# Unused tiles between weight halves, the halves of transposed h and the arena

## The chip, the cores and the metric

The kernel runs on one core of one Trainium2 chip. The metric is the device time of one execution in microseconds. Three runs of the kernel before took 504.98 us in the median (504.83 to 505.34).

## The reference

One layer of a hybrid decoder block on 512 tokens of width 1024, in float32. A root-mean-square norm is followed by one input projection, whose columns feed two token mixers side by side: native sparse attention (compressed, selected and sliding branches) and multi-scale retention in chunks of 128. Each mixer's output is gated and projected, the two are merged by sigmoid gates, and an output projection with a second norm is added to the input.

```
h = rms_norm(x, norm_pre)
proj = h @ w_in                      # 1024 x 6936, split into 15 parts
o_a = nsa(q_n, k_c, v_c, k_s, v_s, k_w, v_w, gate_n)
y_a = (o_a * silu(z_n)) @ w_nsa_o
o_b = retention(q_r, k_r, v_r)
y_b = (o_b * silu(z_r)) @ w_ret_o
merged = sigmoid(m_a) * y_a + sigmoid(m_b) * y_b
x = x + rms_norm(merged @ w_out, norm_post)
```

## The kernel before, in words

**Split products.** To keep float32 accuracy with TensorE's faster float32r type, each operand is held as two float32r halves, an upper one (`hi`) and a lower one (`lo`, what is left after the upper one). A product is three matmuls: upper by upper, and the two mixed terms. `mm3` issues them in the order `(ah, bh)`, `(ah, bl)`, `(al, bh)`; the first argument is the stationary operand (the weights loaded into TensorE), the second the moving one.

**Weights.** They come from HBM as one stream of 512 KB pieces into a ring of four `raw` tiles. `splitter` makes two pairs `whi`, `wlo` of [128, 512] of each piece, an upper half by a copy (ScalarE or VectorE), a lower half by a subtraction on VectorE. The pairs lie in a pool of their own, `wts`, with nine buffers of each name.

**h.** `hTh` and `hTl` are the halves of the transposed, scaled input, [128, 8, 512] each, in the pool `hT`. They are written at the beginning and at the end overwritten with merged gates.

**The arena.** `arena_r` is one tile of 70 KB per partition in the pool `big`. Most of what is kept as float32r halves lies in it under names given by `at(kb, n, FR)`: the attention's queries, keys and values, the retention's states, the gated outputs `gah`, `gal`, `gbh`, `gbl`. A second region, outside of the pools, holds plain float32 tiles and is named `words`; where the same bytes are used as float32r, their name is `shorts`. Four sums of h's quarters (`SH`) lie in it, but for the lower half of the fourth, which is in the arena at 40 KB.

**Order of allocation in a partition.** Dynamic-DMA scratch and constants, the region of `words`, then the pools `small`, `const`, `wts` (nine `whi`, then nine `wlo`), `hT` (`hTh`, then `hTl`), `big` (`arena_r`, then `rsrow`), `raw`. Each begins where the one ahead of it ends. That puts the first `whi` at byte 69,056, the first `wlo` at 87,488, `hTh` at 105,920, `hTl` at 122,304, `arena_r` at 138,688 and the first `raw` at 212,416: all of them 448 modulo 512. The region of `words` begins at 2,176, which is 128 modulo 512. All larger pieces within these tiles are multiples of 512 bytes, but for the 280 columns of one block (`WC`).

**The matmul loops.** `nat` has h as stationary operand and 512 columns of a weight block as moving one; `tra` has 128 columns of the weights as stationary and h's or a gated output's 512 tokens as moving one. `product` (for the second halves of the merge gates, computed by seven products instead of eight) works with 256 columns: weight slices stationary, quarters of h or their sums `SH` moving. `pair` and `out_seven` are the same for one projection block and for the output. Attention and retention multiply pieces of the arena with each other. Transposes go through TensorE with an identity as moving operand and the data, in `words`, as stationary one (line 263).

**Order of the work.** The order on every engine is written out ahead of time by a planner: coroutines (`od.spawn`) that offer instructions, and a model of the engines' times that picks the next. It depends on modelled costs alone, not on addresses. The tiles' framework derives the semaphores.

Of the kernel before, what the change touches and what calls it, by code (L numbers as in the profile page):

```python
# [10 lines left out]
FT = mybir.dt.float32  # L11
# [7 lines left out]
P = 128  # L19
# [131 lines left out]
def block_kernel(ctx: ExitStack, tc, x, xT, x0s, ws, small, w2s, norm_post, rope_r, dmask, out):  # L151
# [21 lines left out]
    wp = ctx.enter_context(tc.tile_pool(name="wts", bufs=1))  # L173
    hp_ = ctx.enter_context(tc.tile_pool(name="hT", bufs=1))
    bp = ctx.enter_context(tc.tile_pool(name="big", bufs=1))
# [3 lines left out]
    pp = ctx.enter_context(tc.tile_pool(name="ps", bufs=1, space=PSUM))  # L179
    ctx.enter_context(tc.manual_schedule())  # L180

    arena_r = bp.tile([P, 70 * 256], FR, name="arena_r")

    def at(kb, n, dt=FT):
        o = int(kb * 256)
        if dt == FR:
            return arena_r[:, o:o + n]
        assert o + n <= 42 * 256
        return words(kb, n)
# [27 lines left out]
    def copy_ns(o, i, k=0):  # L217
        return (1.042 if far(i) else 0.521) * size(o) + 69 + 61 * k + part(i, 93)
# [4 lines left out]
    def act(o, i, func=AF.Copy, r=0.0, **kw):  # L223
        S.activation(o, i, func, **kw)  # L224
        return od.op("act", act_ns(o, i, lazy(kw.get("bias"), kw.get("scale"))) + (95 if "accum_out" in kw else 0), r)

    def cp_any(o, i, r=0.0):

        cd = copy_ns(o, i)
        if od.begin("act", r) + act_ns(o, i) <= od.begin("dve", r, near(i)) + cd + DVE_BIAS:  # L230
            return act(o, i, r=r)
        V.tensor_copy(o, i)  # L232
        return od.op("dve", cd, r, near(i))
# [50 lines left out]
    nhalf = cp.tile([P, 4], FT, name="nhalf")  # L284
    G.memset(nhalf, -0.5)

    hTh = hp_.tile([P, KD, SEQ], FR, name="hTh")
    hTl = hp_.tile([P, KD, SEQ], FR, name="hTl")


# [124 lines left out]
    def in_ring(p):  # L415

        return min(p, KD) + max(p - 2 * KD, 0) - sum(min(max(p - 2 * i, 0), 2) for i in sload)
    hook = {}

    def load_next():  # L420
        i = len(raws)
        if i < len(loads):
            raw = rp.tile([P, 1024], FT, name="raw", tag="raw", bufs=NR)
            o, c, r = loads[i][0], 0, parts[2 * (i - NR) + 1][2] if i >= NR else 0.0
            for j, n in enumerate(loads[i][1]):
                if isinstance(o, int):
                    DMA.dma_start(raw[:, c:c + n], ws[o:o + P * n].rearrange("(p n) -> p n", p=P))
                    o += P * n
                else:
                    DMA.dma_start(raw, o)  # L430
                e = od.dma(P * n * 4, r)
                c += n
                if i + j == 0:
                    load_xT(0)
            raws.append((raw, e + (EARLY if 6 <= i < 16 else 0.0)))
            for fn in hook.get(i, ()):
                fn()
# [10 lines left out]
    def splitter():  # L448
        for i, (_, pieces) in enumerate(loads):
            n = sum(pieces)  # L450
            for k in range(2):
                p = 2 * i + k
                late = p - 2 * len(loads) + 8
                own = KD <= p < 2 * KD or late >= 0 or i in sload
                if late >= 0:
                    yield od.need("gb")
                if i in sload:
                    yield od.need(*{2: ("heads",), 1: ("vr0", "vr1"), 0: ("pair1",), 3: ("pair2",)}.get(sload[i], ("sums",)))
                yield lambda: own or in_ring(p) < in_ring(len(done)) + NW
                while len(raws) <= i:  # L460
                    yield lambda: len(raws) > i or len(raws) < NR or len(parts) > 2 * (len(raws) - NR) + 1
                    if len(raws) <= i:
                        load_next()
                r = max(raws[i][1], done[-1] if done and not own else sfree.get(sload.get(i), 0.0))
                yield r, "act"
                m = n // 2
                src = raws[i][0][:, k * m:(k + 1) * m]
                if late >= 0:
                    hi, lo = at(4 * late, 512, FR), at(4 * late + 2, 512, FR)
                elif i in sload:  # L470
                    hi, lo = (a[:, k * 512:(k + 1) * 512] for a in SB[sload[i]])
                elif own:
                    hi, lo = WC[p - KD]
                else:
                    hi = wp.tile([P, 512], FR, name="whi", tag="whi", bufs=NW)
                    lo = wp.tile([P, 512], FR, name="wlo", tag="wlo", bufs=NW)
                vh, vl = hi[:, :m], lo[:, :m]
                if sload.get(i, 0) % 10 == 1:
                    e = act(vh, src, r=r, scale=-1.0)
                elif p:  # L480
                    e = cp_any(vh, src, r)
                else:
                    V.tensor_copy(vh, src)
                    e = od.op("dve", copy_ns(vh, src), r, True)
                od.spawn(split_lo(p, hi, lo, src, vh, vl, e), rank(p))
                nxt[0] = p + 1
                yield

    def split_lo(p, hi, lo, src, vh, vl, r):
        yield lambda: rank(p)() == 0 or od.eng["dve"] <= od.now + SLACK  # L490
        yield r
        if sload.get(p // 2, 0) % 10 == 1:
            r = stt(vl, src, -1.0, f(vh), OP.mult, OP.subtract, r)
        else:
            r = sub_split(vl, src, vh, r)
        yield lambda: len(parts) == p
        parts.append((hi, lo, r))
        if p % 2 and len(raws) <= p // 2 + NR:
            load_next()
# [3 lines left out]
    def rank(p):  # L503

        return lambda: 0 if p <= wanted[0] + (PSOON if p in pairp else SOON) else 4
# [1364 lines left out]
    od.spawn(h_split(), 0)  # L1870
    od.spawn(norms(), 1)
    od.spawn(splitter(), lambda: rank(nxt[0])())
    od.spawn(edges(), 1)
    od.spawn(weight_sums(), 1)
# [111 lines left out]
```

## Time and profile before

| | |
|---|---|
| median of three runs | 504.98 us |
| the profiled execution | 504.99 us, span 503.2 us |
| TensorE (PE) | 493.7 us busy, 98%, 2666 matmuls |
| TensorE weight loads (PEld) | 421.4 us, 84% |
| VectorE (DVE) | 424.6 us, 84% |
| ScalarE (ACT) | 324.7 us, 65% |
| GpSimd (POOL) | 39.3 us, 8% |
| HBM | 249 GB/s over the span |

A row of the table of groups gives line, engine, operation, names (written tile, arrow, read tiles), shapes, count, then busy us, mean ns of one, and idle time ahead of it with what ended it. Matmuls are pipelined and their spans overlap: the mean of one is longer than the step from one start to the next. A row of the timeline gives start and length in us, engine, line, operation, names, shape, and how many instructions are merged in the row.

### The profile page before, as it was taken

The page shows a single profiled execution, that of the slowest core. Times are in us where ns is not written, and L with a number is a line of the kernel's source. Part 1 is how long each engine was busy: PE and PEld are TensorE (multiplying, and loading weights), DVE is VectorE, ACT ScalarE, POOL GpSimd, SP SyncE. Part 2 cuts the span into 40 slices and gives each one's busy share as a digit, 9 for nine tenths or more (in the row PEclk, how much of TensorE's full clock was granted, in tenths as well). Part 3 has the DMA queues.
Part 4 walks back from the last instruction along what each step waited for, and adds up shares of the span by engine and source line. Part 5 has one row for each costly group of instructions (what it writes and reads, how often), then busy time and mean ns, then how long its engine had stood idle before and what let it go on. Part 6 is the DMA issues. An engine that isn't in the chain of part 4 may idle for free.

```text
span 503.2 us, 7872 instructions
## 1 busy us (share of the span) xinstructions
PE 493.7 (98%) x2666; PEld 421.4 (84%) x2666; DVE 424.6 (84%) x996; ACT 324.7 (65%) x722; POOL 39.3 (8%) x66
## 2 busy tenths in 40 slices
PE   8999999999999999999999999999999999999994
PEld 7898887888888888888888888888888989988883
DVE  6698899989989989998789999778787867979795
ACT  6795599558679788784587574835435535527642
POOL 3102100023000210000100000101000000000010
PEclk9999999999999999999999999999999999999999
DMA  8968995779998899325556673530473735635813
GB/s 318 385 211 283 326 227 200 242 136 225 370 238 182 262 293 211 113 85 166 119 173 212 215 235 114 126 126 8 162 250 113 233 116 191 199 113 169 303 56 142
DMA packets 31080, 98.75 MB, mean 196 GB/s; under 512 B 3136, under 2 KB 6976, under 8 KB 30272
## 3 DMA queue, kind: packets, MB, share of 16 engines
q1 hardware_dynamic: 24576, 70.85, 41.5%
q0 software_dynamic: 6320, 27.26, 22.9%
q8 instruction: 21, 0.34, 0.3%
q14 instruction: 19, 0.16, 0.1%
q10 hardware_dynamic: 144, 0.14, 0.1%
HBM read 93.52 MB, written 31.98 MB: 249 GB/s over the span
## 4 chain that ended last, share of the span: by engine, by line
PE 89%; DMA 5%; DVE 4%; issue 1%; ACT 0%; POOLq 0%; DVEq 0%; POOL 0%; ACTq 0%; SPq 0%
PE bank L257 70%; PE bank L1234 8%; PE bank L1725 7%; PE bank L263 4%; DMA raw<-in_stream_dram 3%; DVE arena_r L236 1%; DMA words<-in_xT_dram 1%; DVE wlo L236 1%; DMA words<-in_x_dram 1%; DVE words L236 1%; DVE words L679 0%; DVE words L249 0%; DVE words L243 0%; DVE words L967 0%; DVE whi L232 0%
## 5 line engine op out<-in xcount | busy, mean ns | idle before, releaser
L224 ACT ACTIVATE whi<-raw 128x512 fp32r<-128x512 f32 x177 | 107.0, 627 | 53.4 <-PE bank L257 36.2
L236 DVE TENSOR_TENSOR wlo<-raw,whi 128x512 fp32r<-128x512 f32 x188 | 123.4, 685 | 10.4 <-ACT whi L224 9.5
L257 PE MATMUL bank<-whi,hTh 128*128 128x512 f32 x192 | 74.0, 407 | 0.3 <-ACT hTh L224 0.3
L257 PE MATMUL bank<-arena_r 128*128 128x256 f32 (+2 forms) x328 | 70.7, 335 | 0.7 <-DVE arena_r L236 0.5
L257 PE MATMUL bank<-whi,hTl 128*128 128x512 f32 x192 | 71.2, 391 | 0.0
L257 PE MATMUL bank<-wlo,hTh 128*128 128x512 f32 x192 | 71.0, 390 | 0.0
L224 ACT ACTIVATE arena_r<-bank 128x512 fp32r<-128x512 f32 (+3 forms) x104 | 49.1, 476 | 26.3 <-PE bank L263 25.4
L236 DVE TENSOR_TENSOR arena_r<-bank,arena_r 128x512 fp32r<-128x512 f32 (+3 forms) x104 | 56.0, 542 | 9.6 <-ACT arena_r L224 8.5
L257 PE MATMUL bank<-arena_r,whi 128*128 128x512 f32 (+1 forms) x208 | 63.6, 381 | 0.0
L224 ACT ACTIVATE words<-words,stat 128x128 f32<-128x128 f32 (+3 forms) x105 | 54.1, 546 | 6.6 <-DVE stat L967 4.9
L257 PEld LDWEIGHTS bank<-arena_r 128*128 128x128 f32 x328 | 50.8, 189 | 7.6 <-DVE arena_r L236 1.2
L257 PE MATMUL bank<-hTh,whi 128*128 128x512 f32 (+1 forms) x144 | 52.2, 363 | 0.0
L257 PE MATMUL bank<-hTh,wlo 128*128 128x512 f32 (+1 forms) x144 | 51.4, 357 | 0.0
L257 PE MATMUL bank<-hTl,whi 128*128 128x512 f32 (+1 forms) x144 | 51.1, 355 | 0.0
L257 PEld LDWEIGHTS bank<-arena_r,whi 128*128 128x128 f32 x208 | 38.8, 188 | 7.3
L257 PEld LDWEIGHTS bank<-whi,hTl 128*128 128x128 f32 x192 | 36.2, 188 | 8.0
L257 PEld LDWEIGHTS bank<-whi,hTh 128*128 128x128 f32 x192 | 36.5, 191 | 6.9 <-ACT hTh L224 0.6
L257 PEld LDWEIGHTS bank<-wlo,hTh 128*128 128x128 f32 x192 | 36.1, 188 | 6.3
L257 PE MATMUL bank<-arena_r,wlo 128*128 128x512 f32 x96 | 37.3, 389 | 0.0
L263 PEld LDWEIGHTS bank<-identr,shorts 128*128 128x128 f32 x268 | 30.1, 140 | 8.6 <-DVE arena_r L236 0.9
L224 ACT ACTIVATE words<-words 128x512 f32<-128x512 f32 (+3 forms) x47 | 27.2, 586 | 12.8 <-DVE words L236 8.0
L263 PE MATMUL bank<-identr,shorts 128*128 128x128 f32 x268 | 31.6, 238 | 0.5 <-DVE arena_r L236 0.5
(182 smaller groups left out, 891.0 us busy)
## 6 DMA issues: line engine op xcount, KB each, us to landing
raw<-in_stream_dram SPq DMA_DIRECT2D x73, 512.0 KB, 4.4
pair<-in_stream_dram POOLq DMA_DIRECT2D x6, 1024.0 KB, 11.8
t<-in_stream_dram POOLq DMA_DIRECT2D x6, 1024.0 KB, 17.2
out<-in_stream_dram POOLq DMA_DIRECT2D x6, 1024.0 KB, 17.1
words<-in_x_dram SPq DMA_DIRECT2D x8, 512.0 KB, 6.9
raw<-s SPq DMA_DIRECT2D x8, 512.0 KB, 4.2
raw<-pair SPq DMA_DIRECT2D x8, 512.0 KB, 4.2
raw<-t SPq DMA_DIRECT2D x8, 512.0 KB, 3.6
```

The costliest lines, as they stand in the source:

```text
L224: S.activation(o, i, func, **kw)
L236: (V if e == "dve" else G).tensor_tensor(o, a, b, op=op)
L257: T.matmul(ps, a, b, start=start, stop=stop)
L263: T.transpose(ps, a, idn)
L1234: T.matmul(ps[m], a, b, start=n in first and s + j == 0, stop=n in last and s + j == 5, skip_group_check=True)
L1725: T.matmul(ps[m], a, b, start=n in first and s + i == 0, stop=n in last and s + i == 5, skip_group_check=True)
```

## The change

It allocates tiles that nothing writes or reads, so that what is allocated behind them begins elsewhere: 64 bytes per partition between the `whi` and the `wlo`, 128 ahead of `hTh`, 128 between `hTh` and `hTl`, 128 ahead of `arena_r`. Modulo 512, `whi` stays at 448, `wlo` moves to 0, `hTh` to 128, `hTl` to 256, `arena_r`, `rsrow` and `raw` to 384; `words` stays at 128. All other text of the kernel is the same. `spacer` allocates once per pool, however often it is called.

```diff
+    spaced = set()
+
+    def spacer(pool, n):
+
+        if pool not in spaced:
+            spaced.add(pool)
+            pool.tile([P, n], FT, name=f"room{n}")
+
+    spacer(bp, 32)
     arena_r = bp.tile([P, 70 * 256], FR, name="arena_r")
...
+    hp_.tile([P, 32], FT, name="room_h")
     hTh = hp_.tile([P, KD, SEQ], FR, name="hTh")
+    spacer(hp_, 32)
     hTl = hp_.tile([P, KD, SEQ], FR, name="hTl")
...
                     hi = wp.tile([P, 512], FR, name="whi", tag="whi", bufs=NW)
+                    spacer(wp, 16)
                     lo = wp.tile([P, 512], FR, name="wlo", tag="wlo", bufs=NW)
```

## The prediction

> **What bounds the kernel now.** I read the page first, from busy shares to the chain of work that ended last, then the table of groups by shape, then the timeline of TensorE alone.
>
> ```profile
> PE 493.7 (98%) x2666; PEld 421.4 (84%) x2666; DVE 424.6 (84%) x996; ACT 324.7 (65%) x722; POOL 39.3 (8%) x66
> PEclk9999999999999999999999999999999999999999
> PE 89%; DMA 5%; DVE 4%; issue 1%; ACT 0%; POOLq 0%; DVEq 0%; POOL 0%; ACTq 0%; SPq 0%
> ```
>
> TensorE is busy 98% of the span at full granted clock and carries 89% of the chain, so the time is the sum of the steps from one matmul to the next. The change adds no instruction, wait or transfer; it can only alter how long instructions take. So the question is whether any instruction's time depends on where its operand starts. In a row, the first name behind the arrow is the moving operand, the second the stationary one.
>
> Where tiles start, worked out from the sizes in order of allocation, in bytes of a partition modulo 512: words and shorts 128; whi, wlo, hTh, hTl, arena and raw all 448. After: words 128, whi 448, wlo 0, hTh 128, hTl 256, arena and raw 384.
>
> The vector engines first, since they already mix starts of 128 and 448:
>
> ```profile
> L236 DVE TENSOR_TENSOR wlo<-raw,whi 128x512 fp32r<-128x512 f32 x188 | 123.4, 685 | 10.4 <-ACT whi L224 9.5 <-PE bank L257 0.4
> L236 DVE TENSOR_TENSOR arena_r<-words,arena_r 128x512 fp32r<-128x512 f32 x15 | 10.1, 682 | 0.0
> L224 ACT ACTIVATE whi<-raw 128x512 fp32r<-128x512 f32 x177 | 107.0, 627 | 53.4 <-PE bank L257 36.2 <-DMA raw<-in_stream_dram 8.2 <-DMA raw<-pair 2.2
> L224 ACT ACTIVATE words<-words 128x512 f32<-128x512 f32 x27 | 16.9, 627 | 5.9 <-DVE words L236 2.8 <-DVE words L249 2.7 <-PE bank L263 0.2
> ```
>
> Three operands at 448 take VectorE 685 ns, a mixture of 128 and 448 takes 682; ScalarE takes 627 in both. I cost the change at nothing there, and these engines have idle time beside TensorE anyway. If that is off by the 3 ns shown, 188 of them are 0.6 us of VectorE time under cover of TensorE; without that cover they would show.
>
> TensorE is another matter. The same shape, 128x256, has two prices:
>
> ```profile
> L257 PE MATMUL bank<-hTh,wlo 128*128 128x256 f32 x48 | 13.6, 283 | 0.0
> L257 PE MATMUL bank<-hTl,whi 128*128 128x256 f32 x48 | 13.6, 282 | 0.0
> L257 PE MATMUL bank<-hTh,whi 128*128 128x256 f32 x48 | 13.6, 282 | 0.0
> L257 PE MATMUL bank<-shorts,whi 128*128 128x256 f32 x112 | 21.0, 277 | 0.0
> L257 PE MATMUL bank<-shorts,wlo 128*128 128x256 f32 x64 | 17.7, 277 | 0.0
> L257 PE MATMUL bank<-arena_r,whi 128*128 128x256 f32 x16 | 4.5, 281 | 0.0
> L257 PEld LDWEIGHTS bank<-shorts,whi 128*128 128x128 f32 x112 | 17.5, 188 | 0.0
> ```
>
> All are issued by `product`, with the same weight slices and kind of output; only the moving operand's place differs. While one matmul streams, the next one's weights are loaded (188 ns), so what can collide is the moving read with the load of the *next* weights. The steps, from the timeline of TensorE (start us, us):
>
> ```profile
> 387.02 0.28 PE L257 MATMUL bank<-hTl,whi 128*128 128x256 f32 x1
> ...
> 388.94 0.28 PE L257 MATMUL bank<-hTh,wlo 128*128 128x256 f32 x1
> ...
> 394.70 0.39 PE L257 MATMUL bank<-shorts,whi 128*128 128x256 f32 x2
> ...
> 395.72 0.39 PE L257 MATMUL bank<-shorts,whi 128*128 128x256 f32 x2
> ...
> 404.05 0.28 PE L257 MATMUL bank<-shorts,whi 128*128 128x256 f32 x1
> ...
> 406.06 0.28 PE L257 MATMUL bank<-shorts,wlo 128*128 128x256 f32 x1
> ```
>
> First pair: moving hTh or hTl at 448, weights at 448, distance 0: 16 steps in 1.92 us, 120.0 ns each. Second pair: shorts at 128, weights at 448, distance 192: 9 steps in 1.02 us, 113.3 ns. Third pair: the fourth weight sum, whose upper half is in words (128) and lower half in the arena (448), so that distances run 192, 0, 192: 17 steps in 2.01 us, 118.2 ns. So distance matters by 6.7 ns, and a sequence that changes distance costs more than the mean of its parts: (2 x 113.3 + 120.0) / 3 = 115.5, measured 118.2, a surcharge of 2.7 ns; over the clean step it is 4.9.
>
> The 512-column matmuls, which are most of the time:
>
> ```profile
> 359.81 0.39 PE L257 MATMUL bank<-arena_r,wlo 128*128 128x512 f32 x1
> ...
> 361.85 0.39 PE L257 MATMUL bank<-arena_r,wlo 128*128 128x512 f32 x1
> 219.72 0.46 PE L263 MATMUL bank<-identr,shorts 128*128 128x128 f32 x4
> 220.02 0.46 PE L257 MATMUL bank<-whi,hTh 128*128 128x512 f32 x1
> 220.32 0.39 PE L257 MATMUL bank<-wlo,hTh 128*128 128x512 f32 x1
> ...
> 222.40 0.39 PE L257 MATMUL bank<-wlo,hTh 128*128 128x512 f32 x1
> ```
>
> At distance 0 throughout, a long run makes 9 steps in 2.04 us: 226.7 ns, twice 113.3, so with no stall left. Right after four transposes (shorts at 128 as weights) the same matmuls make 9 steps in 2.08 us, and only then settle. A run of one distance settles into a clean step; a break in it costs some 0.04 us.
>
> **The change part by part.** *No instruction moves.* A spacer tile is allocated and never touched. Every queue keeps its order; POOL's and SP's DMAs are the same. *The raw tiles* shift by 448 bytes; the page's row for them stays my price:
>
> ```profile
> raw<-in_stream_dram SPq DMA_DIRECT2D x73, 512.0 KB, 4.4
> ```
>
> They still start at a multiple of 64, and the ring runs ahead of the splits, so I cost that at nothing; if a landing became later, ScalarE's splits would be late next (DMA is 5% of the chain).
>
> *Distances after the change*, moving start minus start of the next weights, modulo 512. `nat` (moving whi, wlo, whi; weights hTh, hTh, hTl): 0, 0, 0 becomes 320, 256, 320. `tra` on hTh and hTl: 0, 0, 0 becomes 192, 256, 192. `tra` on the gated halves in the arena: 448, 384, 448. `product` on hTh and hTl: 192, 256, 192; on the first three weight sums: from 192 throughout to 192, 128, 192; on the fourth: from 192, 0, 192 to 192, 384, 192. Attention keeps both operands in the arena, at distance 0. So the constant distance of the 512-column runs, the condition under which they settle, becomes an alternating one. How many they are:
>
> ```profile
> L257 PE MATMUL bank<-whi,hTh 128*128 128x512 f32 x192 | 74.0, 407 | 0.3 <-ACT hTh L224 0.3
> L257 PE MATMUL bank<-hTh,whi 128*128 128x512 f32 x96 | 38.7, 403 | 0.0
> L257 PE MATMUL bank<-arena_r,whi 128*128 128x512 f32 x192 | 59.2, 389 | 0.0
> L257 PE MATMUL bank<-arena_r,wlo 128*128 128x512 f32 x96 | 37.3, 389 | 0.0
> ```
>
> Each of the first two rows stands for a product in three parts (upper by upper, upper by lower, lower by upper): 3 x 192 + 3 x 96 + 192 + 96 = 1152 (the first block's 96, four of one kind in a row, alternate less often; I count them in).
>
> - 512 columns, 1152 of them, now alternating. Bounds: 0 (they settle at 226.7 as before) and 4.9 ns each (the fourth sum against the clean one), 5.6 us; below nothing, the unsettled stretches could go, which is the second rival. I take half the surcharge of 2.7, since a 512-column step leaves room for the 188 ns load that a 113 ns step doesn't: 1.35 x 1152 = +1.6 us.
> - `product` on hTh and hTl, 144 matmuls: from 120.0 towards the fourth sum's pattern, 118.2 if distance 256 acts as 0 does: -0.3 us (113.3 would be -1.0).
> - The first three weight sums, 176 - 32 = 144 matmuls: between 113.3 and 118.2, the middle: +0.35 us (0 to +0.7).
> - The fourth sum, 16 + 32 = 48: loses its zero; 0 to -4.9 ns, the middle: -0.1 us.
> - Attention's arena-by-arena matmuls and the transposes: unchanged.
>
> Sum +1.6. The profiled execution took 504.99 us (span 503.2, so 1.8 outside, which stays), the median of the runs is 504.98: 504.99 + 1.6 = 506.6 us. TensorE's share of the chain, 89%, would take 0.2 off, which I leave in. What a run can tell from no change is about 0.2%, 1.0 us.
>
> The Trainium skill, SBUF — State Buffer, "Who interferes with whom", says that the moving operand and LDWEIGHTS have independent read ports and that TensorE and ScalarE never wait on anyone. By that rule the sum is 0 and the time 505.0. The trace disagrees as far as TensorE goes (120.0 against 113.3 ns at one shape) and agrees for ScalarE (627 and 627 ns).
>
> **The rivals.** *Likeliest, slower:* alternating distance keeps runs from settling, +1.6 us as summed; at the fourth sum's full 4.9 ns, +5.6 + 0.7 - 0.3 = +6.0, 511.0 us. For it speaks the third timeline pair; against it that it was measured at 256 columns only.
>
> *No change:* the 512-column runs settle with alternating distances too, since only the first few steps of a run collide; `product` gives 0.3. 504.7 us. For it speaks that after transposes, whose weights lie elsewhere, nine steps suffice. The rule of ports comes out here as well.
>
> *Faster:* distance 0 is the only bad one, and 256 is as good as 192. Then `product` on hTh and hTl goes to 113.3 (144 x 6.7 = -1.0 us), and runs start settled. The transposes are
>
> ```profile
> L263 PE MATMUL bank<-identr,shorts 128*128 128x128 f32 x268 | 31.6, 238 | 0.5 <-DVE arena_r L236 0.5
> ```
>
> about 67 fours, 67 x 0.04 = 2.7 us at most; half of it, because attention's runs stay at 0: -1.35. Together -2.4, 502.6 us; at most -3.7, 501.3. For it speaks the second pair; against it the third, where a zero in three costs more than its third. It decides from the point where alternating costs a 512-column matmul under 0.3 ns.
>
> **How the numbers follow.** Alternation costs: 0.42, of which 0.06 stays within 0.2%. No change: 0.27. Faster: 0.27. Something else of either sign (landings, the vector engines): 0.04, shared. That makes faster 0.28, same 0.34, slower 0.38. Range: from below the faster case, 502.0, to most of the full surcharge, 510.0; the likeliest case alone runs from 505.5 to 511.0.
>
> **What would show it.** Right: `product` on hTh and hTl near 118 ns a step; the long 512-column run near 360 us at 228 instead of 226.7; mean durations of those groups up from 389. The no-change rival: 226.7 there again. The faster one: 113.3 in `product`, and nine steps after transposes in 2.04 us. VectorE at 685 and ScalarE at 627 in each case; another number there makes my reading of the vector engines wrong. The sum would be wrong in size if attention's arena matmuls changed, which I cost at nothing.

## The result and the profile after

Three runs of the changed kernel took 509.58 us in the median (508.69 to 509.6), against 504.98: 1.0084 times as long, 95% interval 1.0061 to 1.0107. Five more runs, told of below, gave 1.0076 (1.0063 to 1.009). The change costs some 4 us. (A ratio is worked out from the single runs of both kernels, so it can differ a little from the quotient of the medians.) One run of e12 below fell to a granted clock of 0.56 and took 811.68 us; it is left out of that kernel's numbers. The profiled execution took 508.69 us, its span is 506.9 us, 3.7 more than before.

The page of the changed kernel, the busy times, the granted clock and the chain's shares by engine:

```profile
PE 497.2 (98%) x2666; PEld 421.2 (83%) x2666; DVE 425.2 (84%) x996; ACT 325.2 (64%) x722; POOL 39.1 (8%) x66
...
PEclk9999999999999999999999999999999999999998
...
PE 91%; DVE 4%; ACT 2%; issue 1%; DMA 1%; DVEq 0%; POOLq 0%; POOL 0%; ACTq 0%
```

TensorE is busy 3.5 us longer with the same 2666 matmuls. The granted clock does not explain it: its mean is 0.998 before and 0.996 after, and in the group of runs around e11 below the kernel before took 504.99 us at 0.996, the changed one 509.27 us at 0.999. TensorE's weight loads (421.4 before), VectorE (424.6) and ScalarE (324.7) hardly move. The groups by shape (nine lines were added ahead of them, so L257 is now L266, L236 is L245, L224 is L233):

```profile
L245 DVE TENSOR_TENSOR wlo<-raw,whi 128x512 fp32r<-128x512 f32 x188 | 123.7, 685 | 10.2 <-ACT whi L233 9.1 <-PE bank L266 0.4
L233 ACT ACTIVATE whi<-raw 128x512 fp32r<-128x512 f32 x177 | 107.1, 627 | 52.9 <-PE bank L266 37.4 <-DMA raw<-in_stream_dram 5.4 <-PE bank L1246 2.1
...
L266 PE MATMUL bank<-whi,hTh 128*128 128x512 f32 x192 | 73.8, 404 | 0.4 <-ACT hTh L233 0.4
...
L266 PE MATMUL bank<-arena_r,whi 128*128 128x512 f32 x192 | 60.2, 394 | 0.0
...
raw<-in_stream_dram SPq DMA_DIRECT2D x73, 512.0 KB, 4.5
```

VectorE stays at 685 ns, ScalarE at 627, the weight stream's landing at 4.5 us (4.4 before). Among the matmuls some means rise (389 to 394), some fall (407 to 404): a mean holds the pipelined overlap and the waits at breaks. The steps from start to start say more. Three long stretches serve as gauges in all that follows: 48 matmuls of `product` on hTh and hTl, then 72 on the first three sums of h's quarters (`SH`; the prediction calls them weight sums, here they are "the sums"), and later 96 on the gated halves in the arena. TensorE's timeline of the kernel before, the first row of each stretch and the first row behind it:

```profile
386.55 0.28 PE L257 MATMUL bank<-hTh,whi 128*128 128x256 f32 x1
...
392.30 0.29 PE L257 MATMUL bank<-shorts,whi 128*128 128x256 f32 x1
...
400.48 0.28 PE L257 MATMUL bank<-hTh,whi 128*128 128x256 f32 x1
...
436.67 0.39 PE L257 MATMUL bank<-arena_r,whi 128*128 128x512 f32 x1
...
458.43 0.39 PE L1725 MATMUL bank<-whi,arena_r 128*128 128x512 f32 x1
```

and of the changed kernel, with two rows from the long 512-column stretch near 365 us ahead:

```profile
364.31 0.39 PE L266 MATMUL bank<-arena_r,wlo 128*128 128x512 f32 x1
...
366.39 0.39 PE L266 MATMUL bank<-arena_r,wlo 128*128 128x512 f32 x1
...
388.81 0.28 PE L266 MATMUL bank<-hTh,whi 128*128 128x256 f32 x1
...
394.37 0.28 PE L266 MATMUL bank<-shorts,whi 128*128 128x256 f32 x1
...
402.87 0.28 PE L266 MATMUL bank<-hTh,whi 128*128 128x256 f32 x1
...
439.27 0.62 PE L266 MATMUL bank<-arena_r,whi 128*128 128x512 f32 x2
...
461.45 0.62 PE L1737 MATMUL bank<-whi,arena_r 128*128 128x512 f32 x2
```

`product` on hT: 5.75 us by 48 is 119.8 ns before, 5.56 us is 115.8 after. The sums: 8.18 us by 72 is 113.6, now 8.50 us, 118.1. The gated halves: 21.76 us by 96 is 226.7, now 22.18 us, 231.0; near 365 us nine steps take 2.08 us, 231.1 each, where they took 2.04. Those steps repeat as 229, 236, 228 to the end of the stretch and do not settle.

A step runs from one matmul's start to the next one's and so holds any wait between them. Adding the steps of all matmuls by kind, after less before, places the whole 3.7 us of the span: 512 columns through `mm3` (1152) +2.13; 512 columns issued in `pair` and `out_seven` with weights as moving operand (288) +1.19; all four sums +0.66; `product` on hT -0.53; attention's arena matmuls -0.05; all else +0.29. The +2.13 is a net: over the steps under 250 ns, `nat` goes from 228.5 to 230.7 ns in the mean, `tra` on hT from 229.6 to 231.6, the gated halves from 226.7 to 231.1, together +3.0 us, while the longer steps, which hold the waits and breaks, came out 0.9 us shorter.

### The profile page after: what moved, and what is told of

Same layout as the page of the kernel before. It is cut to its first block, busy times and chain, and to the rows that moved or that the text cites. A ratio compares the mean times of both kernels' runs of the same rounds, so it can differ in the third digit from the quotient of the medians.

```text
span 506.9 us, 7872 instructions
## 1 busy us (share of the span) xinstructions
PE 497.2 (98%) x2666; PEld 421.2 (83%) x2666; DVE 425.2 (84%) x996; ACT 325.2 (64%) x722; POOL 39.1 (8%) x66
## 4 chain that ended last, share of the span: by engine, by line
PE 91%; DVE 4%; ACT 2%; issue 1%; DMA 1%; DVEq 0%; POOLq 0%; POOL 0%; ACTq 0%
PE bank L266 73%; PE bank L1246 8%; PE bank L1737 7%; PE bank L272 4%; DVE arena_r L245 1%; ACT words L233 1%; DVE wlo L245 1%; DMA words<-in_x_dram 1%; DVE words L245 1%; DVE words L979 0%; ACT whi L233 0%; DVE words L691 0%; ACT arena_r L233 0%; DVE words L258 0%; DVE words L252 0%
## 5 line engine op out<-in xcount | busy, mean ns | idle before, releaser
L233 ACT ACTIVATE whi<-raw 128x512 fp32r<-128x512 f32 x177 | 107.1, 627 | 52.9 <-PE bank L266 37.4
L245 DVE TENSOR_TENSOR wlo<-raw,whi 128x512 fp32r<-128x512 f32 x188 | 123.7, 685 | 10.2 <-ACT whi L233 9.1
L266 PE MATMUL bank<-whi,hTh 128*128 128x512 f32 x192 | 73.8, 404 | 0.4 <-ACT hTh L233 0.4
L266 PE MATMUL bank<-whi,hTl 128*128 128x512 f32 x192 | 71.8, 394 | 0.0
L266 PE MATMUL bank<-arena_r 128*128 128x256 f32 (+2 forms) x328 | 70.7, 335 | 0.6 <-DVE arena_r L245 0.5
L266 PE MATMUL bank<-wlo,hTh 128*128 128x512 f32 x192 | 71.2, 391 | 0.0
L233 ACT ACTIVATE arena_r<-bank 128x512 fp32r<-128x512 f32 (+3 forms) x104 | 49.1, 477 | 27.1 <-PE bank L272 26.1
L245 DVE TENSOR_TENSOR arena_r<-bank,arena_r 128x512 fp32r<-128x512 f32 (+3 forms) x104 | 56.0, 541 | 10.7 <-ACT arena_r L233 9.5
L266 PE MATMUL bank<-arena_r,whi 128*128 128x512 f32 (+1 forms) x208 | 64.6, 386 | 0.0
L233 ACT ACTIVATE words<-words,stat 128x128 f32<-128x128 f32 (+3 forms) x105 | 54.1, 545 | 6.7 <-DVE stat L979 4.9
L266 PEld LDWEIGHTS bank<-arena_r 128*128 128x128 f32 x328 | 50.9, 189 | 7.6 <-DVE arena_r L245 0.8
L266 PE MATMUL bank<-hTh,whi 128*128 128x512 f32 (+1 forms) x144 | 52.2, 363 | 0.0
L266 PE MATMUL bank<-hTl,whi 128*128 128x512 f32 (+1 forms) x144 | 51.2, 355 | 0.0
L266 PE MATMUL bank<-hTh,wlo 128*128 128x512 f32 (+1 forms) x144 | 51.0, 354 | 0.0
L266 PEld LDWEIGHTS bank<-arena_r,whi 128*128 128x128 f32 x208 | 38.9, 188 | 7.6
L266 PEld LDWEIGHTS bank<-whi,hTl 128*128 128x128 f32 x192 | 36.0, 188 | 8.5
L266 PEld LDWEIGHTS bank<-whi,hTh 128*128 128x128 f32 x192 | 35.9, 188 | 7.2 <-ACT hTh L233 0.7
L266 PEld LDWEIGHTS bank<-wlo,hTh 128*128 128x128 f32 x192 | 36.2, 189 | 6.8
L266 PE MATMUL bank<-arena_r,wlo 128*128 128x512 f32 x96 | 37.6, 392 | 0.0
L233 ACT ACTIVATE words<-words 128x512 f32<-128x512 f32 (+3 forms) x47 | 27.2, 586 | 12.7 <-DVE words L245 7.7
```

The costliest lines, as they stand in the source:

```text
L245: (V if e == "dve" else G).tensor_tensor(o, a, b, op=op)
L266: T.matmul(ps, a, b, start=start, stop=stop)
```

## Experiments

Two theories stood at the start. A, the prediction's: a constant distance between moving operand and next weights lets a run settle, an alternating one doesn't. B: at 512 columns every distance but 0 costs, constant or not. Each kernel below is the kernel before with the edit shown. Beside them the kernel before took 505.1, 505.35, 505.29 and 505.2 us in the four groups of runs; a ratio is against the runs of its group, with its 95% interval. Distances from here on are modulo 256, for a reason that the third experiment gives.

**One constant distance of 192 (e1).**

```diff
+    hp_.tile([P, 48], FT, name="room_h")
     hTh = hp_.tile([P, KD, SEQ], FR, name="hTh")
```

> One spacer of 192 bytes ahead of hTh and no other: whi and wlo stay at 448, hTh, hTl, arena and raw move to 128 modulo 512, where words lies already. Distances (moving start minus start of the next weights) are then constant within each loop: nat 320, tra and product 192, attention 0. Theory A (what costs is a distance that alternates from one matmul to the next): the long 512-column run of the gated halves settles at 226.7 ns a step, product on hTh and hTl goes from 120.0 to 113.3 ns (144 matmuls, -1.0 us), the fourth sum from 118.2 to 113.3 (-0.2 us): about 503.8 us, below the kernel before. Theory B (any distance other than 0 costs a 512-column matmul): 1152 matmuls at some +4.4 ns, less 1.2 us at 256 columns: about 509 us.

508.07 us, ratio 1.0062 (1.0049 to 1.0074). Its timeline, the same gauges:

```profile
389.73 0.28 PE L257 MATMUL bank<-hTh,whi 128*128 128x256 f32 x1
...
395.18 0.28 PE L257 MATMUL bank<-shorts,whi 128*128 128x256 f32 x1
...
403.34 0.28 PE L257 MATMUL bank<-hTh,whi 128*128 128x256 f32 x1
...
439.02 0.62 PE L257 MATMUL bank<-arena_r,whi 128*128 128x512 f32 x2
...
461.41 0.62 PE L1726 MATMUL bank<-whi,arena_r 128*128 128x512 f32 x2
```

At the constant distance of 192, `product` on hT falls to 113.5 ns (5.45 us by 48), as hoped for 256 columns. The gated halves, at the same constant 192, rise to 233.2 (22.39 us by 96), more than in the changed kernel with its mixture. Theory A falls, B stands. What is best for 256 columns is bad for 512. A fourth stretch is used from here on, 48 matmuls of `out_seven` with h's tiles as stationary operand and weights as moving one, as in `nat`. In e1 they stand at a constant 64:

```profile
466.92 0.39 PE L1726 MATMUL bank<-whi,hTh 128*128 128x512 f32 x1
...
477.90 0.39 PE L1726 MATMUL bank<-whi,arena_r 128*128 128x512 f32 x1
```

10.98 us by 48 is 228.8 ns, where the kernel before took 226.7.

**Only the 64 bytes between whi and wlo (e2).**

```diff
                     hi = wp.tile([P, 512], FR, name="whi", tag="whi", bufs=NW)
+                    if not spaced:
+                        spaced.append(wp.tile([P, 16], FT, name="room_w"))
                     lo = wp.tile([P, 512], FR, name="wlo", tag="wlo", bufs=NW)
```

> Only the 64 bytes between whi and wlo: whi at 448, wlo, hTh, hTl, arena and raw at 0. nat has 448, 0, 448; tra and the gated halves 64, 0, 64; the first three weight sums 192, 128, 192. Theory A (alternation): all 1152 pay as in the changed kernel, some +4.4 ns each, sums +0.7 us: 509 to 510 us. Theory B (distance other than 0): two of three pay, about +3.4 us, sums +0.7: 509 us, but the step at distance 0 stays 226.7. Rival C (the spacing of h and the arena is what costs, the weight halves are harmless): 505 us.

509.86 us, ratio 1.0096 (1.0081 to 1.0112). One spacer of 64 bytes costs as much as all four spacers of the change. All that is allocated behind it shifts by 64 as well, so that of three matmuls on the gated halves two stand at 64 and one at 0 (229.3 ns on average), and in `nat` and the stretch of `out_seven` two at 192 and one at 0:

```profile
467.38 0.40 PE L1728 MATMUL bank<-whi,hTh 128*128 128x512 f32 x1
...
478.63 0.40 PE L1728 MATMUL bank<-whi,arena_r 128*128 128x512 f32 x1
```

11.25 us by 48 is 234.4 ns. Both theories had given about this time; that the weight halves would be harmless falls.

**256 bytes at the same place (e3).** The same edit with 64 words instead of 16.

> 256 bytes between whi and wlo in place of 64: whi at 448, wlo, hTh, hTl, arena and raw at 192. nat has 256, 0, 256; tra and the gated halves 256, 0, 256; sums 192, 448, 192. If the pattern of places repeats every 256 bytes, 256 is as 0: the 512-column runs settle at 226.7, product on hTh and hTl stays at 120.0, and only the sums pay, at most +0.7 us: 505.0 to 505.7 us. If it repeats every 512 bytes or later, theory A gives 509 to 510 us, as with 64 bytes.

504.9 us, ratio 0.9995 (0.9986 to 1.0004). The gated halves in its timeline:

```profile
436.48 0.62 PE L258 MATMUL bank<-arena_r,whi 128*128 128x512 f32 x2
...
458.24 0.62 PE L1728 MATMUL bank<-whi,arena_r 128*128 128x512 f32 x2
```

21.76 us, 226.7 ns. An unused tile as such costs nothing, and a distance of 256 is as good as 0: the pattern repeats every 256 bytes as far as this shows.

**Only the 128 bytes between hTh and hTl (e4).**

```diff
     hTh = hp_.tile([P, KD, SEQ], FR, name="hTh")
+    hp_.tile([P, 32], FT, name="room_l")
     hTl = hp_.tile([P, KD, SEQ], FR, name="hTl")
```

> Only 128 bytes between hTh and hTl: whi, wlo, hTh at 448, hTl, arena and raw at 64. nat has 0, 384, 0; tra on h 0, 128, 0; the gated halves 128 throughout; first three sums 192 throughout as before. Theory A (alternation): nat and tra on h pay, 864 x 4.4 ns = 3.8 us, the long run of the gated halves settles at 226.7: about 508.5 us. Theory B (distance other than 0): the gated halves pay (288 x 4.4), and one in three of nat and tra (288 x 4.4): +2.5 us, 507.5 us, with the long run of the gated halves near 231.

510.13 us, ratio 1.0101 (1.0087 to 1.0114). The arena shifts with it: gated halves at a constant 128 take 233.3 ns. Theory B had given 507.5: `pair` and `out_seven`, which it did not count, add 1.5 us by the steps, the sums 0.7, and the gated halves cost 0.6 more than reckoned. Its timeline has one thing that no theory asked for:

```profile
389.59 0.28 PE L257 MATMUL bank<-hTh,whi 128*128 128x256 f32 x1
...
395.24 0.28 PE L257 MATMUL bank<-shorts,whi 128*128 128x256 f32 x1
...
403.72 0.28 PE L257 MATMUL bank<-hTh,whi 128*128 128x256 f32 x1
```

`product` on hT, now at 0, 128, 0, takes 117.7 ns. The sums behind it stand where they stood, at a constant 192, and still take 117.8 (8.48 us by 72) instead of 113.6.

**All tiles from the weights on moved together by 64, words not (e5).**

```diff
+    wp.tile([P, 16], FT, name="room_w")
     arena_r = bp.tile([P, 70 * 256], FR, name="arena_r")
```

> One spacer of 64 bytes ahead of whi: whi, wlo, hTh, hTl, arena and raw all move together, from 448 to 0 modulo 512; words stays at 128. All distances among them stay 0, only the weight sums go from 192 to 128. Relative theory (the price of a 512-column matmul goes by the distance modulo 256 of moving operand and next weights, 0 being free): 512-column runs settle at 226.7 as before, the first three sums leave 113.3 for at most 120: 505.0 to 506.0 us. Absolute theory (the place itself counts, 448 being the good one): 512-column steps rise as in the changed kernel, 509 us.

505.67 us, ratio 1.0002 (0.9993 to 1.0012). The rows of the sums and of the gated halves:

```profile
393.58 0.28 PE L258 MATMUL bank<-shorts,whi 128*128 128x256 f32 x1
...
402.13 0.28 PE L258 MATMUL bank<-hTh,whi 128*128 128x256 f32 x1
...
438.74 0.40 PE L258 MATMUL bank<-arena_r,whi 128*128 128x512 f32 x1
...
460.51 0.39 PE L1726 MATMUL bank<-whi,arena_r 128*128 128x512 f32 x1
```

At distance 0 the gated halves stay at 226.8 ns although whi, wlo, h's halves and the arena all lie elsewhere; the sums, whose distance went from 192 to 128, take 118.8. It is the distance that counts, not the place.

**Only the 128 bytes ahead of the arena (e6).**

```diff
+    bp.tile([P, 32], FT, name="room_a")
     arena_r = bp.tile([P, 70 * 256], FR, name="arena_r")
```

> Only the 128 bytes ahead of the arena: whi, wlo, hTh, hTl stay at 448, arena and raw at 64 modulo 512. nat and tra on h keep distance 0, the gated halves have 128 throughout, attention 0, the first three sums 192 with the addresses of before. Relative theory: only the gated halves (288 at some +6.6 ns) and the merged gates with weights (about 140 at some +5) pay: +2.6 us, 507.6 us; nat stays at 226.7. On the sums, which run at 117.7 ns in the kernel with 128 bytes between hTh and hTl although their addresses are those of before: if what came ahead of them (a product at alternating distance) is the cause, 113.3 here; if the place of raw and arena, and so the traffic of the other engines, is, 117.7 here too.

509.12 us, ratio 1.006 (1.0042 to 1.0079). Gated halves at 128: 233.3 ns (22.40 us by 96). The stretch of `out_seven` with h's tiles, untouched, ran 226.9. The time expected was 507.6. The gated halves, `pair` and `out_seven` cost 2.7 us by the steps, as reckoned; another 1.2 us of its profile lie in the first 96 matmuls of `nat`, which keep distance 0. They ran from 4.89 to 28.84 us instead of 4.71 to 27.42, and why stays open. The sums took 113.6 here, so the arena's place was not what slowed them in e4. What differs there is the stretch ahead of them, `product` at mixed distances.

**Constant 32 and constant 224 (e7, e8).** As in e1, with 8 and with 56 words.

> One spacer of 32 bytes ahead of hTh: distances constant, tra, product and the gated halves +32, nat -32, attention 0, sums as before. If the price grows evenly with distance between 0 (nothing) and 64 (nat at 229.0 ns, +2.3): about +1.2 ns on 1152, 506.4 us. If half a line of 64 bytes is worse than a whole one (the single weight load 32 bytes off in the kernel before is followed by a step of 235): +8 ns on 1152, 514 us.

> One spacer of 224 bytes ahead of hTh: distances constant, tra, product and the gated halves 224 modulo 256 (that is -32), nat +32. The mirror image of the kernel with 32 bytes. If only the size of the distance counts, the same time as there; if its sign counts too (192 costs 6.8 ns, 64 only 2.3), nat and tra change places and the times differ: the loops at +32 would be the cheaper ones.

511.39 us, ratio 1.0115 (1.01 to 1.013), and 511.37 us, 1.0113 (1.0096 to 1.0131). The gated halves at 32:

```profile
441.66 0.62 PE L257 MATMUL bank<-arena_r,whi 128*128 128x512 f32 x2
...
464.05 0.63 PE L1726 MATMUL bank<-whi,arena_r 128*128 128x512 f32 x2
```

22.39 us, 233.2 ns; 233.3 at 224. The smallest step away from 0 that was tried costs the full price, in either direction; neither 506.4 nor 514 us, the times expected for e7, came out.

**Words at distance 0 too, the sums kept at 192 (e9).** The prediction laid the unsettled steps after transposes on the transposes' weights, which lie elsewhere. If so, this should beat both kernels.

```diff
-    nc.alloc_sbuf_tensor("room", [P, 58 * 256], FT)
-    low, made = nc.sbuf_base - 58 * 1024, {}
+    nc.alloc_sbuf_tensor("room", [P, 58 * 256 + 64], FT)
+    low, made = nc.sbuf_base - 58 * 1024 - 192, {}
...
-        v = [words(4 * i, 1024, FR) for i in range(7)] + [at(40, 1024, FR)]
+        v = [words(4 * i - 1 / 16, 1024, FR) for i in range(7)] + [at(40, 1024, FR)]
```

> The region of words moves 64 bytes up, everything behind it by 256, so that words come to distance 0 from all other tiles (modulo 256); the weight sums alone are taken 64 bytes lower, which keeps them at distance 192. Nothing else changes. Distance 0 as the free one for 512 columns: the matmuls that stream while the weights of a transpose (words) load now take 230 to 238 ns and come down to 226.7, some 68 x 7 ns = -0.5 us, and the runs after transposes start settled, up to -2.7 us: 502.2 to 504.8, most likely 504. If the load of a transpose's weights unsettles a run for another reason than its place (its 128 columns, its PSUM bank): 505.3, no change. Weight sums at 113.3 ns by both.

505.14 us, ratio 0.9999 (0.999 to 1.0008). No gain. Its timeline, nine steps after four transposes at two places, from the second matmul at the first and from the third at the other (from the second it is 2.08 us there, too):

```profile
220.06 0.40 PE L257 MATMUL bank<-wlo,hTh 128*128 128x512 f32 x1
...
222.10 0.39 PE L257 MATMUL bank<-wlo,hTh 128*128 128x512 f32 x1
...
270.55 0.40 PE L1234 MATMUL bank<-wlo,arena_r 128*128 128x512 f32 x1
...
272.63 0.39 PE L1234 MATMUL bank<-wlo,arena_r 128*128 128x512 f32 x1
```

2.04 us at the first place, where the kernel before took 2.08; 2.08 at the second, where the kernel before took 2.04 by its steps. At the 23 places where at least eleven 512-column matmuls follow transposes, these nine steps take 2.065 us in the mean before and 2.068 here. So the place of the transposes' weights is not what unsettles a run. A break does it without any transpose: behind twelve 256-column matmuls of attention, all in the arena, the kernel before takes 236, 228, 233 and 230 ns from 240.43 us. Whether the place of the identity, which streams in a transpose, adds to it isn't tested; e9 leaves it as it was against all tiles but words.

**The same tiles as in e5 moved by 192 (e10).** With 48 words instead of 16: words come to distance 0, and the sums with them.

> 192 bytes ahead of the first weight tile: all tiles but words move by 192 and come to distance 0 from words, the weight sums included. Weight sums from 113.3 to 120.0 ns: 144 x 6.7 = +1.0 us and the fourth sum from 118.2 to 120.0, +0.1. With the gain at transposes as in the run beside it (-0.5 to -2.7 us): 503.8 to 506; without it 506.4. If the sums stay at 113.3, a distance of 0 at 256 columns isn't what costs 120.0, and the place of hTh and hTl is.

506.85 us, ratio 1.003 (1.0018 to 1.0041), 1.6 us more than before. The sums:

```profile
392.92 0.28 PE L258 MATMUL bank<-shorts,whi 128*128 128x256 f32 x1
...
401.56 0.28 PE L258 MATMUL bank<-hTh,whi 128*128 128x256 f32 x1
```

8.64 us by 72 is 120.0 ns: distance 0 is the costly one at 256 columns, in words as in hT. By the steps of its profile the sums cost +1.0 us, as foreseen. Its first 60 us hold 0.5 us more of waits than before, which no distance explains; the reason stays open.

**The changed kernel in more rounds (e11), and a constant 128 (e12).** e12 is e1 with 32 words.

> The changed kernel again, in more rounds, so that its price is known to better than 1 us: by the steps of its profile (226.7 to 232 ns and mixtures of 229 on 1152 matmuls, product and sums as measured) 509.0 to 509.6 us, ratio 1.0085. Is the distance the only cause, its unsettled runs look the same again: 229 to 236 ns near 365 us.

> 128 bytes ahead of hTh, all else as before: one constant distance of 128 modulo 256 in every 512-column product with weights or h, and in product on hTh and hTl. If only distance 0 is free at 512 columns: 233.3 ns everywhere in them, 1152 x (233.3 - 228) = +6.1, product on hT near 119, sums 113.3 as before: 511.3. If the place of the arena or alternation carries part of the price (the kernels with one spacer of 128 cost 3.0 and 5.1 us): 508 to 510.

The changed kernel: 509.19 us, ratio 1.0076 (1.0063 to 1.009), gated halves 231.0 ns again. Its second profile has a span of 507.4 us, and the 1152 matmuls of `mm3` take +2.79 us there, against +2.13 in the first; `pair` and `out_seven` +1.18, sums +0.67, `product` -0.53; the steps under 250 ns of the 1152 cost +3.0 us as in the first. The constant 128: 510.53 us, ratio 1.0105 (1.009 to 1.0121).

```profile
391.03 0.28 PE L257 MATMUL bank<-hTh,whi 128*128 128x256 f32 x1
...
396.73 0.28 PE L257 MATMUL bank<-shorts,whi 128*128 128x256 f32 x1
...
441.39 0.62 PE L257 MATMUL bank<-arena_r,whi 128*128 128x512 f32 x2
...
463.78 0.63 PE L1726 MATMUL bank<-whi,arena_r 128*128 128x512 f32 x2
```

`product` on hT 118.8 ns, gated halves 233.2. A constant distance of 128 costs more than the change's mixture of 192, 128 and 192 does in the same stretch.

## Why the prediction was right or wrong

It said slower by 1.6 us, and the kernel is slower by some 4. That it gets slower, that TensorE's steps alone do it, and that `product` on hT gains while the 512-column matmuls and the first three sums lose, held. The size and the mechanism did not. The direction was luck in part: by the prediction's mechanism a constant distance would have cost nothing, and constant distances of 32, 128 and 224 cost more than the change does (e7, e12, e8). The change slows the kernel because most distances it makes at 512 columns are not 0. The range had room for 509.58 us only because it allowed for most of the full surcharge.

- *The count.* 1152 left out 288. In `pair` and `out_seven`, 512-column matmuls are issued by lines of their own, not through `mm3`. The groups of the changed kernel:

```profile
L1246 PE MATMUL bank<-whi,arena_r 128*128 128x512 f32 x64 | 20.4, 399 | 0.0
L1246 PE MATMUL bank<-wlo,arena_r 128*128 128x512 f32 x32 | 12.5, 392 | 0.0
L1737 PE MATMUL bank<-whi,arena_r 128*128 128x512 f32 x32 | 10.0, 395 | 0.0
L1246 PE MATMUL bank<-whi,hTh 128*128 128x512 f32 x24 | 9.6, 401 | 0.0
...
L1737 PE MATMUL bank<-wlo,arena_r 128*128 128x512 f32 x16 | 6.3, 394 | 0.0
```

  64 + 32 + 32 + 16, and six rows of 24 like the one shown, are 288; they cost 1.2 us, which the sum lacked as a whole. (The other 48 of `out_seven` take their moving operand from the arena and cost 0.1 us.)

- *The price at 512 columns.* Taken: 1.35 ns, half the surcharge of the fourth sum. Measured over the 1152: 2.13 us, 1.8 ns (2.4 in the second profile); without the steps of 250 ns and more, 3.0 us and 2.6 ns in both; and 4.1 over the 288. The 1152 pay less than the 288. Many of them stand just behind a break, where they were unsettled before: `nat` took 228.5 ns and `tra` on hT 229.6 in the mean before, 230.7 and 231.6 after, where settled runs go from 226.7 to 231.0. And `nat`, at 64, 0, 64 after the change, settles lower in some runs (227.7 ns in the one from 249.82 us). The argument for halving, that a longer matmul leaves room for the load, had no row behind it; a settled run lost 4.3 ns, near the full 4.9.

- *The mechanism.* Constant against alternating was the wrong distinction at 512 columns: constant distances of 32, 128, 192 and 224 cost 6.5 ns, more than the mixture. The right one at 512 columns is 0 against anything else, 64 paying least (2.1 ns in e1). The prediction's faster rival had it the other way around: it took distance 0 as the bad one, from rows of 256 columns, where it is. The mistake in both was to carry a rule from 256 columns to 512.

- *The breaks.* The reading that runs after transposes start unsettled because of where the transposes' weights lie fell with e9, and with it the reason given for "a break in it costs some 0.04 us".

- *The smaller terms.* `product` on hT: 115.8 ns instead of 118, -0.53 us instead of -0.3. The first three sums: 118.1, the upper end of what was given, +0.65 us instead of +0.35. The fourth sum, costed at -0.1 us, stayed as it was (117.8 ns over its 24 matmuls before, 118.0 after). Attention's arena matmuls at nothing: -0.05 us in one profile, +0.15 in the other, as costed. VectorE, ScalarE, landings: as costed.

The rule in the Trainium skill that by itself would have given no change (SBUF — State Buffer, "Who interferes with whom": independent read ports for the moving operand and the weight load) does not give what was measured at either size: 226.7 against 233.2 ns and 113.5 against 120.0 for the same work at other distances. No run shows where the two reads meet.

No version beat the kernel before. Its layout already holds distance 0 in the 1440 matmuls of 512 columns and 192 in the sums; only `product` on hT stands badly, and its moving tiles are those of the 512-column products. Moving them gains 0.9 us there (e1) and loses more.

## What to carry to other kernels

When TensorE is the bound, list the start addresses of moving operands and of the next weights modulo 256 for each long run, and look at start-to-start steps: equal starts were best at 512 float32r columns, 192 apart at 256 columns, and 3% and 6% lay between good and bad. An unused tile of 256 bytes was free (e3). One of 32 or 64 bytes cost 1% where it moved operands of the same matmuls against each other (e7, e2), and nothing measurable where it moved nearly all of them together (e5). Count a shape over all lines that issue it before multiplying a price, and take the price from a row of that very shape.

## What the hardware showed that was not expected

Steps in ns, from the three gauges and the stretch of `out_seven` with h's tiles, by distance (moving start minus start of the next weights, modulo 256):

| distance | 512 columns | 256 columns |
|---|---|---|
| 0 | 226.7 (before, e3), 226.8 (e5) | 119.8 (before), 120.0 (e10) |
| 32 | 233.2 (e7), 233.3 (e8) | 117.9 (e7) |
| 64 | 228.8 (e1, `out_seven`) | |
| 128 | 233.2 (e12), 233.3 (e4, e6) | 118.8 (e5, e12) |
| 192 | 233.2 (e1) | 113.3 to 113.8, but 117.8 (e4, sums) |
| 224 | 233.3 (e7, e8) | 118.1 (e8) |
| 192, 128, 192 | 231.0 (after) | 118.1 (after) |
| 192, 0, 192 | 234.4 (e2) | 115.8 (after), 118.2 (before, fourth sum) |

- At distance 0 the steps after a break run through one sequence, 229 233 236 224 231 236 228 233 230 227 227 ns, entered at different points, and then stay at 227, 226. At 128 (e12) they alternate 229, 238 for good. That looks like two streams that slip past each other until they no longer meet, which only some distances allow. It is an argument; no run shows what they meet at.
- History can matter: the sums at an unchanged distance of 192 ran at 117.8 for 72 steps when what came ahead of them was mixed (e4), and at 113.3 to 113.8 otherwise. At 512 columns one distance can hold two steps as well: in e1, `nat` at a constant 64 ran 20 steps in 4.59 us, 229.5 ns, and later 20 in 4.67 us, 233.5, both behind attention's matmuls:

```profile
215.02 0.39 PE L257 MATMUL bank<-whi,hTh 128*128 128x512 f32 x1
...
219.61 0.40 PE L257 MATMUL bank<-whi,hTl 128*128 128x512 f32 x1
...
250.54 0.40 PE L257 MATMUL bank<-whi,hTh 128*128 128x512 f32 x1
...
255.21 0.40 PE L257 MATMUL bank<-whi,hTl 128*128 128x512 f32 x1
```

  So the distance modulo 256 decides much, but not alone; the two numbers for 192, 0, 192 at 256 columns say the same.
- Left open: why 0 is free at 512 columns and the costliest at 256; why 64 is mostly cheap where 192 isn't; and whether it is the next weights' load or one still further ahead that collides, since every layout that was run changes them together.
